# Experts of a mixture in plain fp32 on 32-column tiles of TensorE, 96 places each, in place of split operands on the whole array

## The chip, the cores and the metric

The kernel runs on one core of one Trainium2 chip. The metric is the device time of one execution in microseconds, the median of three. The engines are named as the profile names them: PE is TensorE (PEld its weight loads), DVE VectorE, ACT ScalarE, POOL GpSimd, SP SyncE, which issues the weights' DMAs. All data is float32.

## The reference, cut to what matters

The model has three transformer blocks over 256 tokens of width 1024. The change is in the mixture of experts that ends the second block. Each token takes its two best experts of eight; each expert is a SwiGLU with 3584 hidden units, so `w_in[e]` is 1024 x 7168 (29.4 MB) and `w_out[e]` is 3584 x 1024 (14.7 MB), 352 MB for all eight.

```python
def moe_swiglu(x, w_router, w_in, w_out):
    logits = (xt @ w_router).astype(jnp.float32)
    top_val, top_idx = lax.top_k(logits, TOP_K)
    top_w = jax.nn.softmax(top_val, axis=-1)
    gates = jnp.sum(jax.nn.one_hot(top_idx, N_EXPERTS, dtype=jnp.float32) * top_w[..., None], axis=1)
    y = jnp.zeros_like(xt)
    for e in range(N_EXPERTS):
        y = y + gates[:, e:e + 1] * swiglu(xt, w_in[e], w_out[e])   # (silu(gate) * up) @ w_out
```

With the inputs that are timed the eight experts are chosen by 41, 50, 89, 65, 58, 72, 59 and 78 tokens.

## The kernel before

All large products are made of split operands: a float32 operand x is written as a float32r part h (ACT, L92) and the rest l = x - h (DVE, L93), and x·w becomes h·wh + h·wl + l·wh, three matmuls at TensorE's float32r rate (L161, L162, L164). The weights are split on the core too. `weights` asks for a piece of 1 MB on SP's queue (L108; four buffers `wr` in the pool `raw`), ACT and DVE split it in halves into `wh` and `wl` (four buffers each), and `linear` multiplies. The activations are the stationary operand (128 tokens), the weights are the moving one (512 columns), and the sums stand in the PSUM pool `mm` (three banks). A second PSUM pool, `ps` (five banks), serves everything else.

`moe` first routes: it gives each token a place in its experts' lists, and `pick` makes a 0/1 matrix P of tokens by places. For two experts at a time, `gather` collects the tokens with P as the moving operand (L1028, 2 x 128 places) into `xgh` and `xgl`; `back` transposes P (L1039). Then `expert` runs on 128 places. For each 512 hidden units it makes gate and up, ACT takes silu of the gate (L932), DVE multiplies by up (L934), and TensorE transposes the result (L209, four times 128x128), which is split into `eh` and `el`. The product with `w_out` follows in two halves of 512 columns; each half's result is split into `f`, given back to the tokens by `back`'s transpose (L1077, four matmuls a half) and added to y by DVE (L1078, and L1080 for the statistics after the last expert). The next pair's gather is put into the second expert of a pair, after its second block of hidden units (`midway`). Expert 0's first 512 hidden units are computed over all tokens (`dense`), since they need no list.

A loop at the end (L1102, L1103) repeats the experts for places from 128 on; its count is read from memory, and is 0 for the lists above. The third block begins behind it. The Tile scheduler orders the instructions of each engine; SP's weight loads are in program order.

Of the kernel before, what the change touches and what calls it, by code (L numbers as in the profile page):

```python
# [21 lines left out]
NEG = -1e30  # L22


class K:
    """Shared pools and the operations that several blocks use."""
# [55 lines left out]
    def load(self, dst, src):  # L82
        """A load in the queue of the weights, after those asked for before."""
# [63 lines left out]
            # the short group first, so that the last ones leave the first tile most time ahead of the second  # L147
# [53 lines left out]
    def transpose_split(self, src, t, out, c0, n, pool=None):  # L201
        """Columns 128*c0.. of the token tile src [128, 128 n], into out[c][0|1][:, t]."""
# [11 lines left out]
    def split_tokens(self, x, n=8, pool=None):  # L214
        """x: [128, 2, 128 n] token-major; the split feature-major operand."""
# [11 lines left out]
    def rstd(self, out, var, eps, scale=1.0):  # L227
        """(scale var + eps) ** -0.5 of a few numbers per partition."""
# [26 lines left out]
    def normalize(self, r, stats, eps, gb, out):  # L255
        """out = the normalized rows of r, whose statistics were taken per 512 columns."""
# [11 lines left out]
    def residual_norm(self, x, alpha, eps, gb, out):  # L268
        """Gives evac(t, c0, n, psum) that adds alpha x and after the last columns normalizes."""
# [14 lines left out]
    def ffn(self, xs, w_in, w_out, hidden, make):  # L284
        """(silu(gate) * up) @ w_out, the products handed to what make gives."""
# [27 lines left out]
    def exps(self, sc, rmax, out, ssum):  # L313
        """out = exp(sc - rmax), summed along the row."""
# [22 lines left out]
    def softplus(self, x, shape):  # L337
        """max(x, 0) + log1p(exp(-|x|)), of a few numbers; log1p(e) = log(1 + e) e / ((1 + e) - 1)."""
# [65 lines left out]
def dsa(k, xs, sm, w_in, kv_norm_w, w_uk, w_uv):  # L404
    """The attention over the keys that the index scores choose; its output token-major."""
# [3 lines left out]
    # index keys (on both halves of the partitions) and queries, feature-major  # L409
# [7 lines left out]
    # w_uk with its ranks on the partitions  # L417
# [12 lines left out]
    # normalized latents, feature-major  # L430
# [13 lines left out]
    # keys of the heads, feature-major; values, token-major  # L444
# [23 lines left out]
    # queries, feature-major, scaled  # L468
# [3 lines left out]
    # the keys that each query doesn't attend to: 1  # L472
# [35 lines left out]
    for h8 in range(0, 16, 8):  # L508
        # slope (key - query) [query, head, key - query tile + 128]
# [12 lines left out]
def conv_taps(k, conv_w, conv_b):  # L522
    """Taps and bias with the channels on the partitions."""
# [11 lines left out]
def ssd_conv(k, xs, w_in, cw, xc, half):  # L535
    """silu(causal convolution) of x (half 0), or B and C (half 1), feature-major: eight chunks each."""
# [14 lines left out]
def ssd(k, sm, xc, sz, dt_bias, a_log, d_skip, norm_w):  # L551
    """The scan over two chunks of 128, gated by sz and normalized; token-major."""
# [4 lines left out]
    # dt = softplus(raw + bias) = max(., 0) + log1p(exp(-|.|)), a = -exp(a_log) dt  # L557
# [11 lines left out]
    # running sums within each chunk, and the sum of the first chunk on all partitions  # L569
# [28 lines left out]
    # state after the first chunk, per group [state, 4 heads x 64]  # L598
# [75 lines left out]
def memory_xattn(k, xs, kt, v, w_mq, w_mo, evac, values):  # L674
# [47 lines left out]
    # the four pairs of heads, one stage apart  # L722
# [13 lines left out]
def hybrid_layer(k, x, a):  # L736
    """The first block; x token-major, as its result is."""
# [12 lines left out]
    # dt, c_kv and the weights of the index heads  # L750
# [44 lines left out]
def retention(k, xs, w_in, w_out, evac):  # L795
    """Retention over the whole sequence at once: (q k^T * decay) v per head, normalized and gated."""
# [22 lines left out]
    # decayed scores, keys on the partitions: keys 0..127 x 256 queries, keys 128..255 x 128 queries  # L819
# [37 lines left out]
def stick_breaking(k, xs, w_kv, w_q, w_out, evac):  # L857
    """Stick-breaking attention, keys on the partitions."""
# [34 lines left out]
        # z less the sums of softplus over the keys from each one on  # L893
# [23 lines left out]
def expert(k, xg, w_in, w_out, hidden, evac, first=None, midway=None):  # L917
    """One expert on 128 tokens; evac(c0, n, psum). first, if given, makes the first 512 hidden units;
    midway is called in between."""
    nc = k.nc  # L920
    n = hidden // 128
    hs = []
    for i in range(0, n, 16):
        hs.append(tuple(k.operand(m, 16) for m in ("eh", "el")))
    if first:
        first(hs[0])
    for c0 in range(512 if first else 0, hidden, 512):
        sg = k.w(2, [512], F32, "esg")

        def gate_up(t, c, m, p):  # L930
            if c < hidden:
                nc.scalar.activation(sg, p, AF.Silu)  # L932
            else:
                nc.vector.tensor_tensor(sg, sg, p, op=OP.mult)  # L934
                a = c0 // 128
                k.transpose_split(sg, 0, hs[a // 16], a % 16, 4)

        k.linear(xg, w_in, [[(c0, 512), (hidden + c0, 512)]], gate_up, tiles=1)
        if midway and c0 == 512:
            midway()  # L940
    k.linear([tuple(v[:, :, c % 16] for v in hs[c // 16]) for c in range(n)], w_out, [(0, 512), (512, 512)],
             lambda t, c, m, p: evac(c, m, p), tiles=1)


def moe(k, x, xs, w_router, w_in, w_out, y, before_rest):
    """Adds the gated experts' results to y; each expert works on the tokens sent to it, 128 at a time.
    Gives the statistics of y per 512 columns."""
# [3 lines left out]
    iota = k.load_rows(k.inp["c_iota"], 1, "iota")  # L951
# [4 lines left out]
    # router  # L956
# [19 lines left out]
    # chosen: fewer than two greater logits (of equal ones the first counts as greater)  # L976
# [19 lines left out]
    # place of each token in its experts' lists (far beyond them where it isn't chosen), list lengths  # L996
# [12 lines left out]
    more = small("more", (1,), I32)  # L1009
    nc.vector.tensor_scalar(more, over, 128.5, 8.0, op0=OP.is_gt, op1=OP.mult)  # L1010

    # the tokens in two parts
# [4 lines left out]
    def pick(P, o, col, off):  # L1017
        """P[token, t, o + i] = 1 where the token's place is off + i."""
        for t in range(2):
            nc.vector.tensor_scalar(P[:, t, o:o + 128], iota[:, off:off + 128], col(t), None, op0=OP.is_equal)  # L1020

    def gather(P, n):
        xg = [k.act8(F32R, m) for m in ("xgh", "xgl")]
        for c in range(8):
            p = k.ps.tile([128, 2, 256], F32, name="ps")
            for i in range(2):
                for t in range(2):
                    nc.tensor.matmul(p[:, i, :n], xt[i][:, t, c * 128:c * 128 + 128], P[:, t, :n],  # L1028
                                     start=(i == 0 and t == 0), stop=(t == 1), skip_group_check=True)
            nc.scalar.copy(xg[0][:, c, :n], p[:, 0, :n])  # L1030
            nc.vector.tensor_copy(xg[1][:, c, :n], p[:, 1, :n])
        return xg

    def back(P, o):
        """The transpose of P, [place, token]."""
        pt = k.w(1, [2, 128], F32R, "pback")
        p = k.ps.tile([128, 2, 128], F32, name="ps")
        for t in range(2):
            nc.tensor.transpose(p[:, t], P[:, t, o:o + 128].bitcast(F32), ident)  # L1039
# [473 lines left out]
```

## Time and profile before

| what | value |
|---|---|
| runs | 2670.33, 2671.1 (median), 2671.24 us |
| profiled execution | span 2671.5 us, which is its whole time |
| PE busy, of the span | 98% |
| DVE, ACT busy | 72%, 57% |
| granted TensorE clock, mean of the span | 0.989 |
| HBM read | 623.55 MB |
| first sparse matmul of the experts, last of `w_out` | starts 1420.2 us, 2399.36 us |

The profiled execution stands 0.4 us above the median of the runs. "Busy" counts the time in which at least one instruction of the engine was under way; the matmuls are pipelined, so the time that a stream of them takes is read from the distance of their starts and not from one record's length. A plain float32 matmul is recorded as two records, a float32r one as one.

### The profile page before, as it was taken

The numbers are of one execution on the slowest core, as the hardware profiler recorded it, in microseconds if no ns is written. First come the engines' busy times: TensorE is split into PE (matmuls) and PEld (weight loads), VectorE is DVE, ScalarE is ACT, GpSimd is POOL, SyncE is SP. The second block draws the span as 40 slices with busy tenths as digits, with TensorE's granted clock in tenths as the row PEclk, the third lists the DMA queues.
The fourth block names the chain that finished last, engine by engine and source line by source line (L and its number), as shares of the span: only waits on it lengthen the run. The fifth ranks groups of instructions, "written<-read, shape, count | busy, mean of one in ns | idle before, by whom it ended". The sixth has DMA issues, their size and how long they took to land. (4 is left out here: it accounts for less than half of the span.)

```text
span 2671.5 us, 34975 instructions
## 1 busy us (share of the span) xinstructions
PE 2614.5 (98%) x13305; PEld 2169.4 (81%) x13305; DVE 1933.7 (72%) x2516; ACT 1533.3 (57%) x1987; POOL 60.2 (2%) x82
## 2 busy tenths in 40 slices
PE   8999999999999999999999999999999999998999
PEld 7889888888787987887978888888888888776777
DVE  4555758765555556555478999989999999888665
ACT  4434445444443344443567777777777777765553
POOL 0000000000000000000000000000000000001100
PEclk9999989999999999999999999999999999998999
DMA  7555414453556844655528999999999999987513
GB/s 253 182 168 190 168 49 166 159 188 126 193 180 205 226 158 158 201 181 187 177 95 283 357 340 358 365 356 339 363 360 338 369 359 361 362 309 240 191 64 110
DMA packets 335279, 630.10 MB, mean 236 GB/s; under 512 B 24431, under 2 KB 43136, under 8 KB 334848
## 3 DMA queue, kind: packets, MB, share of 16 engines
q1 hardware_dynamic: 332896, 624.59, 67.3%
q10 hardware_dynamic: 2208, 3.21, 0.9%
q8 instruction: 106, 1.74, 0.3%
q14 instruction: 69, 0.57, 0.1%
HBM read 623.55 MB, written 4.19 MB: 235 GB/s over the span
## 5 line engine op out<-in xcount | busy, mean ns | idle before, releaser
L93 DVE TENSOR_TENSOR wl<-wr,wh 128x1024 fp32r<-128x1024 f32 x1158 | 1374.0, 1218 | 433.2 <-ACT wh L92 404.6
L92 ACT CAST wh<-wr 128x1024 fp32r<-128x1024 f32 x1158 | 1191.2, 1049 | 633.5 <-PE mm L164 454.1
L161 PE MATMUL mm<-wh,xh 128*128 128x512 f32 (+2 forms) x1264 | 492.5, 390 | 7.7 <-ACT xh L92 5.1
L164 PE MATMUL mm<-wh,xl 128*128 128x512 f32 (+2 forms) x1264 | 487.9, 386 | 5.7 <-DVE xl L93 5.7
L162 PE MATMUL mm<-wl,xh 128*128 128x512 f32 (+2 forms) x1264 | 486.8, 386 | 3.8 <-DVE wl L93 3.7
L161 PE MATMUL mm<-wh,xgh 128*128 128x512 f32 x880 | 323.6, 397 | 0.8 <-ACT esg L932 0.5
L162 PE MATMUL mm<-wl,xgh 128*128 128x512 f32 x880 | 322.5, 394 | 0.0
L161 PEld LDWEIGHTS mm<-wh,xh 128*128 128x128 f32 x1264 | 241.0, 191 | 55.5 <-ACT xh L92 8.4
L164 PEld LDWEIGHTS mm<-wh,xl 128*128 128x128 f32 x1264 | 241.0, 191 | 53.6 <-DVE xl L93 8.9
L162 PEld LDWEIGHTS mm<-wl,xh 128*128 128x128 f32 x1264 | 240.8, 191 | 51.7 <-DVE wl L93 8.4
L164 PE MATMUL mm<-wh,xgl 128*128 128x512 f32 x880 | 275.4, 391 | 0.0
L161 PEld LDWEIGHTS mm<-wh,xgh 128*128 128x128 f32 x880 | 165.3, 188 | 50.4 <-ACT esg L932 17.2
L164 PEld LDWEIGHTS mm<-wh,xgl 128*128 128x128 f32 x880 | 165.6, 188 | 34.0
L162 PEld LDWEIGHTS mm<-wl,xgh 128*128 128x128 f32 x880 | 165.5, 188 | 31.9 <-DVE wl L93 0.5
L191 PE MATMUL mm<-xh,wl 128*128 128x256 f32 x648 | 185.7, 287 | 1.4 <-DVE wl L93 1.4
L189 PE MATMUL mm<-xh,wh 128*128 128x256 f32 x648 | 185.9, 287 | 1.2 <-DVE xc L545 0.4
L190 PE MATMUL mm<-xl,wh 128*128 128x256 f32 x648 | 185.5, 286 | 0.4 <-DVE xl L93 0.4
L162 PE MATMUL mm<-wl,eh 128*128 128x512 f32 x448 | 175.0, 391 | 1.1 <-DVE wl L93 1.1
L161 PE MATMUL mm<-wh,eh 128*128 128x512 f32 x448 | 175.6, 392 | 0.0
L164 PE MATMUL mm<-wh,el 128*128 128x512 f32 x448 | 174.7, 390 | 0.0
L189 PEld LDWEIGHTS mm<-xh,wh 128*128 128x128 f32 x648 | 125.6, 194 | 2.2 <-PE ps L209 0.6
L191 PEld LDWEIGHTS mm<-xh,wl 128*128 128x128 f32 x648 | 125.7, 194 | 2.1 <-DVE wl L93 2.0
(450 smaller groups left out, 2922.8 us busy)
## 6 DMA issues: line engine op xcount, KB each, us to landing
wr<-moe_w_in SPq DMA_DIRECT2D x440, 512.0 KB, 6.3
wr<-moe_w_out SPq DMA_DIRECT2D x112, 1024.0 KB, 7.2
wr<-ffn_w_in SPq DMA_DIRECT2D x66, 1024.0 KB, 5.1
wr<-w_in SPq DMA_DIRECT2D x50, 1024.0 KB, 5.1
wr<-ffn_w_out SPq DMA_DIRECT2D x30, 1024.0 KB, 5.1
wr<-ret_w_in SPq DMA_DIRECT2D x24, 1024.0 KB, 5.6
wr<-w_mkv SPq DMA_DIRECT2D x8, 1024.0 KB, 5.0
wr<-w_out SPq DMA_DIRECT2D x8, 1024.0 KB, 5.0
```

Of the source, the lines that this page charges most:

```text
L92: self.nc.scalar.copy(H, src)
L93: self.nc.vector.tensor_tensor(L, src, H, op=OP.subtract)
L161: nc.tensor.matmul(p, h, wh[:, c:c + m], start=first, stop=False)
L162: nc.tensor.matmul(p, h, wl[:, c:c + m], start=False, stop=False)
L164: nc.tensor.matmul(acc[t][i][:rows, :m], l, wh[:, c:c + m], start=False, stop=last)
L189: nc.tensor.matmul(o, wh[:, s], h, start=first, stop=False, skip_group_check=True)
L190: nc.tensor.matmul(o, wh[:, s], l, start=False, stop=False, skip_group_check=True)
L191: nc.tensor.matmul(o, wl[:, s], h, start=False, stop=(k == kn - 1), skip_group_check=True)
```

## The change

Experts have 96 places (`CAP`), in three groups of 32. Inside an expert nothing is split: the gathered tokens `xg`, the hidden units `eh` and the weights are plain float32, and TensorE takes the weights from the DMA's buffer `wr`. A group's 32 places are the stationary operand of a 32-column tile of the array, and the four column tiles at (0, 32j) multiply the same places by four different pieces of the weights: of `w_in` two halves of the gate and two of up, of `w_out` two halves of the columns in each of two row chunks. One matmul into all four tiles is called a set of four below; a piece of 1 MB has three sets, one a group. Sums alternate between three banks of `mm` and three of `ps`; an expert begins with `mm`, has one more accumulator for each 1024 hidden units, and one for `w_out`.

Pieces of `w_in` are 128 rows with 1024 gate and 1024 up columns, in DRAM rows of 4 KB (before: 2 KB); the last half block has 2 KB rows. Pieces of `w_out` are two chunks of 128 rows with all 1024 columns, rows of 4 KB (before 2 KB).

silu and the product now put gate and up, which are on different partitions, together; the transposes are 64 rows by 128 (`turn`, L946), 42 in an expert where there were 28. At an expert's end `evac` adds the two row chunks' sums per group: an ACT copy and two DVE additions of 32x512. Then all 96 places are split (96x1024) and given back with eight matmuls (L1138), as before. Hi and lo products of the gather are summed in PSUM. The loop for longer lists is there twice, for places from 96 and from 192.

```diff
+def expert(k, xg, o, w_in, w_out, hidden, evac, first=None, midway=None):
...
+    def accumulators():
+        banks[0] += 1
+        if banks[0] % 2:
+            return [k.mm.tile([128, 512], F32, name="mm") for _ in range(groups)]
+        return [k.ps.tile([128, 512], F32, name="ps") for _ in range(groups)]
+
+    def turn(g, h, c0, sub):
...
+        for c in range(m):
+            nc.tensor.transpose(p[:, c], h[0:64, c * 128:c * 128 + 128], ident[0:64, 0:64])
+        dst = hidden_units(c0 // 128, 2 * m)[:, :, g * 32:g * 32 + 32].rearrange("p (s c) t -> p c s t", s=2)
+        nc.vector.tensor_copy(dst, p.rearrange("p c (s t) -> p c s t", s=2))
...
+        for c in range(8):
...
+            k.mark = nc.sync.dma_start(raw, src)
+            for g in range(groups):
+                for j in range(4):
+                    nc.tensor.matmul(acc[g][32 * j:32 * j + 32, :sub], xg[:, c, o + 32 * g:o + 32 * g + 32],
+                                     raw[:, j // 2, j % 2 * sub:j % 2 * sub + sub], start=(c == 0), stop=(c == 7),
+                                     tile_position=(0, 32 * j), skip_group_check=True)
+            if c == 3:
+                for f in pend:
+                    f()
+                pend = []
+        for g in range(groups):
+            h = k.wl.tile([128, 1024], F32, name="wl")[:, :512]
+            nc.scalar.activation(h[64:128, :sub], acc[g][0:64, :sub], AF.Silu)
+            nc.vector.tensor_tensor(h[0:64, :sub], h[64:128, :sub], acc[g][64:128, :sub], op=OP.mult)
+            pend.append(partial(turn, g, h, c0, sub))
...
     def run(xg, o, wi, wo, pt, g, last, first=None, midway=None):
...
+            nc.scalar.copy(odd[:64], p[64:128])
+            for c in range(2):
+                nc.vector.tensor_tensor(res[32 * i:32 * i + 32, c], odd[32 * c:32 * c + 32], p[32 * c:32 * c + 32], op=OP.add)
...
+        k.split(f[0][:CAP], f[1][:CAP], made[0][:CAP])
...
+    for r in range(2):
+        k.mark = None
+        n = nc.values_load(more[0:1, r:r + 1], min_val=0, max_val=8)
+        with tc.For_i(0, n, 1) as e:
```

The first place is the end of an expert on PE. Before, in the middle of the product with `w_out`, whose first half of columns is given back between matmuls of the second half:

```order
L161 MATMUL mm<-wh,eh 128x512 [waits Activation_49]
L162 MATMUL mm<-wl,eh 128x512 [waits DVE_49]
L1077 MATMUL ps<-f,pback 128x512 [waits Activation_49]
L1077 MATMUL ps<-f,pback 128x512 [waits PE_49]
L164 MATMUL mm<-wh,el 128x512
L161 MATMUL mm<-wh,eh 128x512
L162 MATMUL mm<-wl,eh 128x512
L164 MATMUL mm<-wh,el 128x512
L161 MATMUL mm<-wh,eh 128x512
L1077 MATMUL ps<-f,pback 128x512 [waits DVE_49]
L1077 MATMUL ps<-f,pback 128x512
```

Now, from the last piece of `w_out` (L983, `mm<-wr,eh`) to the next expert's second piece of `w_in` (L962, `mm<-wr,xg`):

```order
L983 MATMUL mm<-wr,eh 32x512 [waits DMAHW4_49]
L983 MATMUL mm<-wr,eh 32x512 x11
L962 MATMUL mm<-wr,xg 32x512 [waits DMAHW5_49,DVE_49,Activation_49]
L962 MATMUL mm<-wr,xg 32x512 x3
L962 MATMUL mm<-wr,xg 32x512 [waits DVE_49,Activation_49]
L962 MATMUL mm<-wr,xg 32x512 x3
...
L962 MATMUL mm<-wr,xg 32x512 [waits DMAHW6_49]
L1138 MATMUL ps<-wh,pback 128x512 [waits Activation_49]
L1138 MATMUL ps<-wh,pback 128x512 x2
L1138 MATMUL ps<-wl,pback 128x512 [waits DVE_49]
...
L962 MATMUL mm<-wr,xg 32x512 x11
```

Each group's first set of the next expert waits until ACT and DVE have taken the group's old sums out of the same bank; the whole result is given back behind the first matmul, of one tile alone, of the second piece.

The second place is the transposes on PE, between two blocks of hidden units. Before:

```order
L161 MATMUL mm<-wh,xgh 128x512
L162 MATMUL mm<-wl,xgh 128x512 [waits DVE_49]
L161 MATMUL mm<-wh,xgh 128x512
L209 MATMUL ps<-c_ident,esg 128x128 [waits DVE_49]
L209 MATMUL ps<-c_ident,esg 128x128 x3
L162 MATMUL mm<-wl,xgh 128x512
```

Now:

```order
L962 MATMUL ps<-wr,xg 32x512 [waits DMAHW0_49]
L962 MATMUL ps<-wr,xg 32x512 x11
L946 MATMUL ps<-c_ident,wl 128x64 [waits DVE_49]
L962 MATMUL mm<-wr,xg 32x512 [waits DMAHW1_49,Activation_49]
L962 MATMUL mm<-wr,xg 32x512 x3
L962 MATMUL mm<-wr,xg 32x512 [waits Activation_49]
...
L946 MATMUL ps<-c_ident,wl 128x64 x3
L946 MATMUL ps<-c_ident,wl 128x64 [waits DVE_49]
L946 MATMUL ps<-c_ident,wl 128x64 x2
L962 MATMUL mm<-wr,xg 32x512 [waits DMAHW2_49]
```

The four transposes that stood together between matmuls of the same shape stand, in threes and fours or alone, between sets of tiles. Going through an expert in this way, PE leaves the tiles for whole-array or 64-row work 10 times, 14 times where a gather is in it, and twice in an expert that happens behind a single tile's matmul.

## Rows read from the trace of the kernel before

**Rows 1.** The page: span, and busy time of each engine.
```profile
span 2671.5 us, 34975 instructions
PE 2614.5 (98%) x13305; PEld 2169.4 (81%) x13305; DVE 1933.7 (72%) x2516; ACT 1533.3 (57%) x1987; POOL 60.2 (2%) x82
```
**Rows 2.** A window in the experts: PE, PEld, DVE, ACT, POOL; clock, DMA share, GB/s.
```profile
1900.00:2000.00 100.00, 99.95 (x446) 80.43 (x445) 90.93 (x87) 77.05 (x85) 0.00 (x0) 1.00 1.02 362
```
**Rows 3.** Waits from 1600 to 2370 us (6.2 experts): us, times, longest.
```profile
PEld mm L161 <- ACT esg L932: 15.1, 36, 0.9
SPq L108 <- DVE wl L93: 561.4, 263, 5.2
```
**Rows 4.** Line L161 of the experts: ns min/median/max, first and last start.
```profile
L161 PE MATMUL mm<-wh,xgh x880: 386/390/502, 1420.2 to 2357.3; 128*128 128x512 f32 x176
```
**Rows 5.** PE in order of time: two experts' first `w_out` matmul, the last matmuls.
```profile
2236.14 0.39 PE L161 MATMUL mm<-wh,eh 128*128 128x512 f32 x1
...
2358.39 0.39 PE L161 MATMUL mm<-wh,eh 128*128 128x512 f32 x1
...
2395.74 0.39 PE L162 MATMUL mm<-wl,eh 128*128 128x512 f32 x1
...
2399.36 0.39 PE L164 MATMUL mm<-wh,el 128*128 128x512 f32 x1
```
**Rows 6.** Groups of the experts' stretch: busy us, mean ns, idle before.
```profile
L93 DVE TENSOR_TENSOR wl<-wr,wh 128x1024 fp32r<-128x1024 f32 x662 | 776.2, 1221 | 52.3 <-ACT wh L92 42.9
L92 ACT CAST wh<-wr 128x1024 fp32r<-128x1024 f32 x661 | 675.9, 1053 | 127.5 <-PE mm L164 70.7 <-DMA wr<-moe_w_out 31.2 <-DMA wr<-moe_w_in 16.0
```
**Rows 7.** PE in order of time: plain float32, whole array, 512 columns.
```profile
975.41 2.74 PE L840 MATMUL ps<-rv,rst 128*128 128x512 f32 x6
...
978.22 0.39 PE L162 MATMUL mm<-wl,xh 128*128 128x512 f32 x1
```
**Rows 8.** PE: four column tiles (L1354), then 64-row matmuls (L1371).
```profile
2513.84 0.66 PE L1354 MATMUL ps<-cw,ht 128*16 128x64 f32 x32
2514.43 1.07 PE L1371 MATMUL ps<-kct,qkb 64*128 64x16 f32 x16
```
**Rows 9.** PE: whole-array matmuls before and after two column tiles (L909 to L911).
```profile
1357.15 0.39 PE L164 MATMUL mm<-wh,xl 128*128 128x512 f32 x1
1357.47 0.43 PE L909 MATMUL ps<-sbe,sv 128*64 128x128 f32 x2
...
1362.82 0.38 PE L911 MATMUL ps<-sbe,sv 128*64 128x128 f32 x2
1363.13 0.51 PE L161 MATMUL mm<-wh,yh 128*128 128x512 f32 x1
```
**Rows 10.** PE: transposes between the experts' matmuls.
```profile
1671.08 0.60 PE L209 MATMUL ps<-c_ident,esg 128*128 128x128 f32 x4
1671.44 0.48 PE L162 MATMUL mm<-wl,xgh 128*128 128x512 f32 x1
```
**Rows 11.** Windows where most DMA rows are 4 KB, and 8 KB.
```profile
6.00:9.00 3.00, 2.58 (x13) 2.19 (x11) 1.99 (x3) 2.14 (x4) 0.00 (x0) 1.00 1.05 404
275.00:280.00 5.00, 5.00 (x44) 5.00 (x43) 1.96 (x2) 1.99 (x2) 0.00 (x0) 1.00 1.00 416
```
**Rows 12.** All engines in order of time behind the last `w_out` matmul.
```profile
2399.79 0.58 ACT L92 CAST f<-mm 128x512 fp32r<-128x512 f32 x1 [4.18 <-PE mm L164]
2400.41 0.69 DVE L93 TENSOR_TENSOR f<-mm,f 128x512 fp32r<-128x512 f32 x1 [3.35 <-ACT f L92]
...
2401.91 1.41 DVE L1078 SCALAR_TENSOR_TENSOR moe_y<-ps,gate,moe_y 128x512 f32<-128x512 f32 x2
2403.24 1.28 DVE L1080 BATCH_NORM_STATS2 mstats<-moe_y 128x6 f32<-128x512 f32 x2
...
2408.49 0.28 DVE L260 BATCH_NORM_AGGREGATE mv<-mstats 128x2 f32<-128x12 f32 x2 [3.97 <-issue]
...
2413.39 0.90 PE L209 MATMUL ps<-c_ident,h 128*128 128x128 f32 x3 [11.28 <-DVE h L1227]
```

More of the change, by code (lines that the diff above doesn't have):

```diff
@@ L914, in stick_breaking @@
     k.linear(k.pairs(ys, 8), w_out, blocks(0, 1024), evac)
-def expert(k, xg, w_in, w_out, hidden, evac, first=None, midway=None):
+CAP = 96
+def expert(k, xg, o, w_in, w_out, hidden, evac, first=None, midway=None):
     nc = k.nc
+    ident = k.const_in("ident")
+    groups = CAP // 32
     n = hidden // 128
-    hs = []
-    for i in range(0, n, 16):
-        hs.append(tuple(k.operand(m, 16) for m in ("eh", "el")))
+    hs = [k.u8(F32, "eh")[:, :16 * CAP].rearrange("p (c t) -> p c t", c=16) for _ in range(2)]
+    half = 12 if first else 16
+    hidden_units = lambda c, m=1: hs[c >= half][:, c - half * (c >= half):c - half * (c >= half) + m]
@@ L925, in expert @@
     if first:
[L926 to L939, printed above, removed]
-            midway()
@@ L941, in expert @@
-    k.linear([tuple(v[:, :, c % 16] for v in hs[c // 16]) for c in range(n)], w_out, [(0, 512), (512, 512)],
-             lambda t, c, m, p: evac(c, m, p), tiles=1)
+        first(hidden_units(0, 4))
+    banks = [0]
+    def accumulators():
[4 more added lines that the diff above has]
+    def turn(g, h, c0, sub):
+        m = sub // 128
+        p = k.ps.tile([128, m, 64], F32, name="ps")
+        for c in range(m):
+            nc.tensor.transpose(p[:, c], h[0:64, c * 128:c * 128 + 128], ident[0:64, 0:64])
+        dst = hidden_units(c0 // 128, 2 * m)[:, :, g * 32:g * 32 + 32].rearrange("p (s c) t -> p c s t", s=2)
+        nc.vector.tensor_copy(dst, p.rearrange("p c (s t) -> p c s t", s=2))
@@ new lines, in expert @@
+    pend = []
+    starts = list(range(512 if first else 0, hidden, 1024))
+    for c0 in starts:
+        w = min(1024, hidden - c0)
+        sub = w // 2
+        acc = accumulators()
+        for c in range(8):
+            raw = k.raw.tile([128, 2048], F32, name="wr")[:, :2 * w].rearrange("p (g n) -> p g n", g=2)
+            src = w_in[c * 128:c * 128 + 128].rearrange("p (g n) -> p g n", g=2)[:, :, c0:c0 + w]
+            k.mark = nc.sync.dma_start(raw, src)
[7 more added lines that the diff above has]
+                    f()
+                pend = []
+        for g in range(groups):
[3 more added lines that the diff above has]
+            pend.append(partial(turn, g, h, c0, sub))
+        if midway and c0 == starts[1]:
+            midway()
@@ new lines, in expert @@
+    acc = accumulators()
+    for i in range(0, n, 2):
+        raw = k.raw.tile([128, 2048], F32, name="wr").rearrange("p (g n) -> p g n", g=2)
+        k.mark = nc.sync.dma_start(raw, w_out[i * 128:i * 128 + 256].rearrange("(g p) n -> p g n", p=128))
+        for g in range(groups):
+            for j in range(4):
+                c = i + j // 2
+                nc.tensor.matmul(acc[g][32 * j:32 * j + 32], hidden_units(c)[:, 0, 32 * g:32 * g + 32],
+                                 raw[:, j // 2, j % 2 * 512:j % 2 * 512 + 512], start=(i == 0), stop=(i == n - 2),
+                                 tile_position=(0, 32 * j), skip_group_check=True)
+        if i == 6:
+            for f in pend:
+                f()
@@ L945, in moe @@
+    for g in range(groups):
+        evac(g, acc[g])
 def moe(k, x, xs, w_router, w_in, w_out, y, before_rest):
@@ L950, in moe @@
     ident, tri = k.const_in("ident"), k.const_in("tri")
[L951 removed]
+    iota = k.load_rows(k.inp["c_iota"], 2, "iota")
     low = k.load_rows(k.inp["c_low"], 1, "low")
@@ L1058, in first @@
             k.linear(xs, w, [(hidden, 512)], up)
-            for i in range(2):
-                p = k.ps.tile([128, 4, 128], F32, name="ps")
-                for c in range(4):
+            p = k.ps.tile([128, 4, CAP], F32, name="ps")
+            for c in range(4):
+                for i in range(2):
                     for t in range(2):
-                        nc.tensor.matmul(p[:, c], parts[i][:, t, c * 128:c * 128 + 128], P[:, t, 0:128],
-                                         start=(c == 0 and t == 0), stop=(t == 1), skip_group_check=True)
-                (nc.vector.tensor_copy if i else nc.scalar.copy)(h[i][:, 0, 0:4], p)
+                        nc.tensor.matmul(p[:, c], parts[i][:, t, c * 128:c * 128 + 128], P[:, t, 0:CAP],
+                                         start=(c + i + t == 0), stop=(i + t == 2), skip_group_check=True)
+            nc.scalar.copy(h[:, 0:4], p)
         return first
@@ L1070, in run, with evac @@
     def run(xg, o, wi, wo, pt, g, last, first=None, midway=None):
-        def evac(c, m, p):
-            f = k.w(4, [2, 512], F32R, "f")
-            k.split(f[:, 0], f[:, 1], p)
+        made = []
+        def evac(i, p):
+            if not made:
+                made.append(k.w(4, [2, 512], F32, "res"))
+            res = made[0]
+            odd = k.wh.tile([128, 1024], F32, name="wh")[:, :512]
+            nc.scalar.copy(odd[:64], p[64:128])
+            for c in range(2):
+                nc.vector.tensor_tensor(res[32 * i:32 * i + 32, c], odd[32 * c:32 * c + 32], p[32 * c:32 * c + 32], op=OP.add)
+        expert(k, xg, o, wi, wo, hidden, evac, first, midway)
+        f = [v.tile([128, 1024], F32R, name=m).rearrange("p (c n) -> p c n", c=2) for v, m in ((k.wh, "wh"), (k.wl, "wl"))]
+        k.split(f[0][:CAP], f[1][:CAP], made[0][:CAP])
+        for c in range(2):
             for t in range(2):
```

68 lines of the change are left out of this document (33 added, 35 removed).

## The prediction

> **What bounds the kernel now.** I read the page first: PE is busy for 98% of the span, DVE for 72% [rows 1]. That is an average over three blocks, so the window in the experts comes next: PE is never idle at a granted clock of 1.00, DVE stands at 91%, ACT at 77%, and the DMA engines at a share of 1.02 with 362 GB/s [rows 2]. PE and the weights' stream are both at their end here. The waits show which of the two yields: SP's weight loads wait 561 us of 770 for DVE to free a buffer, while PE's own loads wait 15 us in 6.2 experts for the silu [rows 3]. DVE in turn waits for ACT and ACT for PE [rows 6]: the stream is throttled from behind, and its engines show a full share because 2 KB rows are slow in them, not because nothing more could be asked for. The stage runs from 1420.2 us [rows 4] to the last matmul's start at 2399.36 [rows 5], 979.2 us.
>
> One expert takes 122.2 us without a gather (2358.39 - 2236.14). A float32r matmul of 512 columns has a pitch of 3.62 / 16 = 0.226 us [rows 5]. An expert needs (7 blocks x 8 chunks x 2 + 28 chunks x 2) x 3 = 504 of them: 114.0 us. 28 transposes at 0.36 / 4 = 0.09 [rows 10] to 0.108 (0.09 and the 0.08 us by which the next matmul's start is late) are 3.0, eight combining matmuls 1.8. That leaves 3.4 us of waits and late starts, of which the silu wait is 15.1 / 6.2 = 2.4.
>
> **Matmuls of the experts.** Plain float32 goes at half the columns per record and with two records a matmul: from 975.41 to 978.22 lie six records and one float32r matmul, (2.81 - 0.23) / 6 = 0.43 each, so 0.86 us a matmul [rows 7]. Alone that would be 3.8 times the old pitch. Everything hangs on whether four column tiles run together. L1354 is the only place with four: 16 matmuls of 64 columns, 32 records, take 0.66 us [rows 8]. Each tile's four matmuls would take 4 x 0.107 = 0.43 us by the pitch of rows 7; the rest, 0.23, I take for the last record's run-out. One after another they would take 1.7 us. So four run together, at the full pitch of each as far as so short a piece tells. I take 0.86 us for a set of four. An expert has 3 blocks x 8 pieces x 3 groups and 14 x 3 of `w_out`, 114 sets, and 24 sets of half length: 126 x 0.858 = 108.1 us, 5.9 below before. Expert 0 (no half block) gains 5.4. Sum: 7 x 5.9 + 5.4 = **-46.7 us**.
>
> The Trainium skill, "TensorE: Matmul & The Clock Gate", Part 3 on tiles, gives measured speedups that speak against this: 3.07 for four row tiles and 2.38 for three column tiles of 512 columns. A set would then last 4 x 0.858 / 3.07 = 1.12 us, an estimate, and the sum would be 262 us higher. The trace agrees that tiles overlap and cannot exclude the loss, since its only four-tile piece has 64 columns.
>
> **What PE gets in addition.** 42 transposes of 64 rows for 28 of 128. A 64-row matmul of L1371 takes at most 1.07 / 8 = 0.13 us in its row tile [rows 8], the old transposes 0.09 to 0.108. I take 0.111: 4.7 for 3.0 us, **+13.6** for eight experts (with 0.09 to 0.13: +6 to +20).
>
> Changes of tile shape. Going into two column tiles, the first starts 0.32 us behind a matmul whose pitch is 0.23: 0.09 lost. Coming out, 1363.13 stands about 0.20 behind the start of the second of the last two tile records (0.11 us into their row), where a tile's own pitch is 0.05 to 0.11, and the first matmul's record is 0.12 longer than those behind it (0.51 for 0.39) [rows 9]. So a visit elsewhere costs 0.18 to 0.36 us; I take 0.27. With ten visits an expert and four more for each of three gathers that is 92 x 0.27 = **+24.8** (17 to 33).
>
> A tile left alone. Twice in an expert the scheduler puts other work behind the first matmul of a piece, so one tile works 0.86 us while three stand still: 16 x 0.858 = **+13.7**.
>
> The end of an expert. Experts 1 to 7 have five accumulators, so the sum over `w_out` stands in `mm` and the next expert begins in the same three banks. A group's bank is free after an ACT copy (0.58) and two DVE additions, for which the nearest row is 0.69 for 128x512 [rows 12]; with fewer partitions I leave it near that, 0.67. Groups end 0.86 us apart on PE, but DVE needs 1.34 for each: group 0's set waits 1.92 + 0.2 - 2 x 0.86 = 0.4 us, the next two 0.48 more each, 1.4. Six ends (expert 0 ends in `ps`): **+8.6**. If the silu of ACT or the copies of the transposes get between, it can be 3 us each (+18).
>
> **What goes away.** The splits of weights: 776 us of DVE and 676 of ACT [rows 6] leave engines that are not PE's bound; what PE gets back is only its own waits, at most 8 x 3.4 = **-27.2**. I take it all: blocks alternate between two sets of banks, so a block no longer waits for the silu of the one before, and no weight waits for a split. DVE and ACT now have about 25 us of work in 120, which covers the silu, the copies and the giving back, except at an expert's end.
>
> Sum of the stage: -46.7 + 13.6 + 24.8 + 13.7 + 8.6 - 27.2 = **-13.2 us**, 966 us, 120.6 for an expert without a gather.
>
> **The weights' stream.** 42 pieces an expert at 120.6 us leave 2.87 us for each. 4 KB rows ran at 404 GB/s at a share of 1.05, 8 KB rows at 416 [rows 11]; 1.049 MB / 404 = 2.60 us, 109 us an expert, hidden behind PE. At the old 362 GB/s it is 2.90 us, 121.7 an expert. SP now waits for PE alone, whose piece of 2.57 us of work frees a buffer; three others are under way meanwhile, 7.8 us of stream. If PE were faster this cover would be gone at 109 us.
>
> **The end of the stage**, which nothing hides, since the third block's first matmul on PE waits for the normalized tokens [rows 12]. Before, from the last matmul's start to the last statistics: 2404.52 - 2399.36 = 5.2 us, because the first half of the columns was done earlier. After: the additions end about 3.9 us after the last set's start (six of 0.67 on DVE), the cast 96x1024 takes 1.05, the subtraction 1.22 [rows 6], matmuls 0.4, and all eight operations behind them are still to do, 4 x 0.70 + 4 x 0.64 = 5.4 [rows 12]: 12.0 us, **+6.8**. The second loop's count is read like the first's, for which DVE stood 3.97 us [rows 12]: **+4.0** (0 if the two reads overlap, 5 with what surrounds the branch).
>
> Total: -13.2 + 6.8 + 4.0 = -2.4 against the profiled execution's 2671.5, so 2669.1 in its terms; its 0.4 us above the median of the runs is left out of account but for rounding: **2669 us**. Less than 0.2% of the time, 5.3 us, can't be told from no change.
>
> **Rivals.** (A) The sum above, chance 0.70. Its unknown terms (transposes, visits, ends, the waits that may come back with up to 27 us, loop) give it its own range of 2654 to 2690.
>
> (B) The stream bounds: 4 KB rows stay at 362 GB/s beside PE. Then an expert takes 121.7 us at best, and the stalls of PE at its ends aren't made up for, 1 to 3 us each, since only 4 MB are buffered: 8 x 1.1 and 8 x 2, +25 us, 2694. It speaks for it that the share is already 1.02, against it the windows of rows 11, short ones. It decides from 2.87 us a piece. Chance 0.11.
>
> (C) Visits, single tiles and ends cost nothing, because PE's queue lets sets and other work overlap: 47 us less, 2622; the stream at 109 us an expert wouldn't stop it. Against it stand the late starts of rows 9. Chance 0.10.
>
> (D) Four tiles with four different streams of 512 columns are slower than the pitch of one. If the 0.23 us over 0.43 in L1354 were half contention, a set would last 1.27 times as long, 1.09 us: 29 us an expert, +233, 2902. If the array took no more columns in all than the float32r stream, 512 in 0.226 us, two records of four matmuls would need 1.81 us and the kernel 3600. Rows 8 speak against the second (64 columns each 0.014 us, if spread evenly through 0.44). It is the case in which the change is plainly slower; chance 0.09, most of it near 2900. This is where the rule of the skill above would lead.
>
> **Numbers.** Within (A) I give 0.25 to faster by over 5.3 us, 0.27 to within, 0.18 to slower; (B) is slower but for 0.01, (C) faster, (D) slower: faster 0.35, same 0.28, slower 0.37. The range that leaves out (D) and most of (C), and holds (A) and (B): 2635 to 2705.
>
> **What would show it.** In the new profile: the four records of a set start within some 0.05 us of each other and sets follow at 0.86 us; the experts' `w_out` starts are 119 to 123 us apart; DMA at or above 400 GB/s when SP isn't waiting, and SP's waits named PE; PE's idle time at an expert's end 1 to 2 us, behind DVE's additions; two stretches of "issue" before the aggregation of the statistics, and 12 us from the last set to the last statistics. The prediction is wrong if sets follow more slowly, if PE waits for DMA throughout, or if the visits are much cheaper or dearer than 0.27 us.

## The result, and the profile after

The changed kernel takes 2689.5 us (median of seven runs, 2676.4 to 2697.1), the kernel before 2671.1 beside it: 1.0061 times, 95% interval 1.0042 to 1.0081, so about 16 to 18 us slower. The runs of the changed kernel spread over 21 us where those of before spread over 3; the mean granted clock was 0.989 in the fastest of them and 0.984 in the slowest. The profiled execution has a span of 2690.7 us, 19.2 above [rows 1].

The page's head, and the windows of the experts (the first the whole stage, the second that of [rows 2]):

```profile
span 2690.7 us, 42117 instructions
PE 2597.4 (97%) x18071; PEld 1705.7 (63%) x18071; DVE 1201.7 (45%) x1940; ACT 863.3 (32%) x1302; POOL 60.7 (2%) x82
```

```profile
1418.00:2410.00 992.00, 957.90 (x9147) 328.63 (x9149) 152.40 (x273) 78.43 (x140) 0.00 (x0) 0.99 0.94 348
...
1900.00:2000.00 100.00, 94.90 (x917) 33.55 (x910) 19.42 (x33) 9.23 (x16) 0.00 (x0) 0.97 0.94 347
```

DVE and ACT have little to do now, 19 and 9 of 100 us, as the change says. But PE isn't full any more (95 of 100 us), its granted clock is below 1, and the DMA engines move less than before, 348 GB/s at a share of 0.94 for 362 at 1.02 [rows 2]. Neither TensorE nor the stream is at its end over the whole stage: they wait for each other by turns. The stage lasts 992 us from 1418.0 us, 13 more than before, where I had 966; the rest of the 19 us is behind it.

Where PE stops is in the list of waits of PE over the stage, and in its order of time around the start of one `w_out`:

```profile
PE mm L983 <- DMA wr<-moe_w_out: 18.4, 11, 2.9
PE mm L962 <- DVE res L1129: 6.5, 17, 0.4
PE ps L962 <- DMA wr<-moe_w_in: 4.6, 9, 1.0
```

```profile
1603.28 1.50 PE L962 MATMUL ps<-wr,xg 128*32 128x256 f32 x24 [0.18 <-DMA wr<-moe_w_in]
1604.71 0.71 PE L946 MATMUL ps<-c_ident,wl 64*128 64x64 f32 x8
1605.81 0.62 PE L962 MATMUL ps<-wr,xg 128*32 128x256 f32 x2 [0.39 <-DMA wr<-moe_w_in]
1606.36 0.46 PE L946 MATMUL ps<-c_ident,wl 64*128 64x64 f32 x4
1606.75 5.54 PE L962 MATMUL ps<-wr,xg 128*32 128x256 f32 x94
1612.38 0.70 PE L946 MATMUL ps<-c_ident,wl 64*128 64x64 f32 x3
1615.35 4.13 PE L983 MATMUL mm<-wr,eh 128*32 128x512 f32 x24 [2.27 <-DMA wr<-moe_w_out]
```

The rows with 128x256 are the half block at the end of `w_in`, whose pieces are 512 KB. It runs out at 1613, and the first piece of `w_out` isn't there: PE stands still for 2.3 us. Six of the seven experts after the first have such a pause, of 2.2 to 2.9 us. Over the stage the list has 24.6 us of waits of PE for weights: 18.4 and 4.6 above, and two items of 0.8. What the weights and the clock do is seen in windows (columns as in [rows 2]; the first two within the half block, the fourth in the product with `w_out`, the others the four stretches of the stage in which the clock was low):

```profile
1598.00:1608.00 10.00, 9.44 (x146) 5.04 (x142) 3.25 (x6) 1.33 (x3) 0.00 (x0) 1.00 0.85 273
1602.00:1612.00 10.00, 9.44 (x156) 4.96 (x144) 1.28 (x4) 0.45 (x2) 0.00 (x0) 1.00 0.89 304
...
1614.70:1618.10 3.40, 2.75 (x16) 0.91 (x20) 0.00 (x0) 0.00 (x0) 0.00 (x0) 0.50 0.99 394
1618.20:1628.20 10.00, 10.00 (x95) 3.02 (x91) 0.49 (x2) 0.00 (x0) 0.00 (x0) 1.00 0.99 363
1867.30:1874.10 6.80, 5.51 (x26) 1.37 (x27) 0.00 (x0) 0.00 (x0) 0.00 (x0) 0.50 0.99 402
1993.60:2000.40 6.80, 5.88 (x31) 1.61 (x35) 0.19 (x1) 0.00 (x0) 0.00 (x0) 0.50 0.96 390
2372.50:2375.90 3.40, 3.40 (x20) 1.09 (x16) 0.00 (x0) 0.00 (x0) 0.00 (x0) 0.50 1.02 419
```

In the half block the stream falls to 273 and 304 GB/s. Around the end of four of the six pauses PE is granted its lower clock, 1.2 of 2.4 GHz, for 3.4 to 6.8 us: the three sets from 1615.35 take 4.13 us where three and the run-out take 2.7. TensorE worked for 17.5 us at half speed in these stretches, so they cost some 9 us on top of the waits.

The tail, as [rows 12]:

```profile
2404.47 6.19 PE L983 MATMUL mm<-wr,eh 128*32 128x512 f32 x56
...
2409.62 4.14 DVE L1129 TENSOR_TENSOR res<-wh,mm 32x512 f32<-32x512 f32 x6 [32.29 <-ACT wh L1127]
2414.87 1.22 DVE L93 TENSOR_TENSOR wl<-res,wh 96x1024 fp32r<-96x1024 f32 x1 [1.11 <-ACTq L1164]
2416.98 1.41 DVE L1140 SCALAR_TENSOR_TENSOR moe_y<-ps,gate,moe_y 128x512 f32<-128x512 f32 x2 [0.89 <-PE ps L1138]
...
2420.81 1.27 DVE L1142 BATCH_NORM_STATS2 mstats<-moe_y 128x6 f32<-128x512 f32 x2
2426.49 0.28 DVE L260 BATCH_NORM_AGGREGATE mv<-mstats 128x2 f32<-128x12 f32 x2 [4.01 <-issue]
```

From the end of the last `w_out` matmul (2404.47 + 6.19) to the last statistics (2422.08) it is 11.4 us; before it was 4.8 (2399.75 to 2404.52 [rows 5, 12]).

### The profile page after: what moved, and what is told of

The parts are those of the page before. It is cut to its first block, busy times and chain, and to the rows that moved or that the text cites. A ratio compares the mean times of both kernels' runs of the same rounds, so it can differ in the third digit from the quotient of the medians.

```text
span 2690.7 us, 42117 instructions
## 1 busy us (share of the span) xinstructions
PE 2597.4 (97%) x18071; PEld 1705.7 (63%) x18071; DVE 1201.7 (45%) x1940; ACT 863.3 (32%) x1302; POOL 60.7 (2%) x82
## 3 DMA queue, kind: packets, MB, share of 16 engines
q8 instruction: 145, 2.38, 0.3%
HBM read 623.56 MB, written 4.19 MB: 233 GB/s over the span
## 5 line engine op out<-in xcount | busy, mean ns | idle before, releaser
L93 DVE TENSOR_TENSOR wl<-wr,wh 128x1024 fp32r<-128x1024 f32 x494 | 594.9, 1212 | 381.8 <-ACT wh L92 363.0
L92 ACT CAST wh<-wr 128x1024 fp32r<-128x1024 f32 x494 | 512.2, 1044 | 513.1 <-PE mm L164 382.8
L161 PE MATMUL mm<-wh,xh 128*128 128x512 f32 (+2 forms) x1264 | 491.6, 390 | 9.4 <-ACT xh L92 6.8
L962 PE MATMUL mm<-wr,xg 128*32 128x512 f32 x3072 | 346.8, 594 | 7.8 <-DVE res L1129 6.5
L983 PE MATMUL mm<-wr,eh 128*32 128x512 f32 x2352 | 265.0, 608 | 18.5 <-DMA wr<-moe_w_out 18.4
L161 PEld LDWEIGHTS mm<-wh,xh 128*128 128x128 f32 x1264 | 240.3, 190 | 57.7 <-ACT xh L92 10.3
L962 PE MATMUL ps<-wr,xg 128*32 128x512 f32 (+1 forms) x2880 | 261.0, 494 | 4.8 <-DMA wr<-moe_w_in 4.6
L962 PEld LDWEIGHTS mm<-wr,xg 128*32 128x32 f32 x3072 | 98.3, 110 | 232.6 <-issue 211.5
L983 PEld LDWEIGHTS mm<-wr,eh 128*32 128x32 f32 x2352 | 74.8, 112 | 195.7 <-issue 154.3
L962 PEld LDWEIGHTS ps<-wr,xg 128*32 128x32 f32 x2880 | 95.1, 110 | 135.4 <-issue 86.9
L972 DVE TENSOR_TENSOR wl<-wl,mm 64x512 f32<-64x512 f32 x48 | 33.1, 690 | 228.7 <-ACT wl L971 228.7
L1129 DVE TENSOR_TENSOR res<-wh,mm 32x512 f32<-32x512 f32 x42 | 28.5, 679 | 230.3 <-ACT wh L1127 229.6
```

The lines of the kernel that those rows point to most:

```text
L92: self.nc.scalar.copy(H, src)
L93: self.nc.vector.tensor_tensor(L, src, H, op=OP.subtract)
L161: nc.tensor.matmul(p, h, wh[:, c:c + m], start=first, stop=False)
L962: nc.tensor.matmul(acc[g][32 * j:32 * j + 32, :sub], xg[:, c, o + 32 * g:o + 32 * g + 32], raw[:, j // 2, j % 2 * sub:j % 2 * sub + sub], ...
L972: nc.vector.tensor_tensor(h[0:64, :sub], h[64:128, :sub], acc[g][64:128, :sub], op=OP.mult)
L983: nc.tensor.matmul(acc[g][32 * j:32 * j + 32], hidden_units(c)[:, 0, 32 * g:32 * g + 32], raw[:, j // 2, j % 2 * 512:j % 2 * 512 + 512], s ...
```

## The experiments

The question was where the 26 us lie by which the stage exceeds my sum: in TensorE's own work, or in weights that come late. Stage times below run from the first tile matmul to the start of the last record of `w_out`, in each run's profile. The distances of experts are those of the first matmuls of their `w_out`, as in [rows 5].

**TensorE's own pace.** Every second piece of weights is not loaded.

```diff
-            raw = k.raw.tile(...)
...
-            k.mark = nc.sync.dma_start(raw, src)
+            if c % 2 == 0:
+                raw = k.raw.tile(...)
...
+                k.mark = nc.sync.dma_start(raw, src)
...
+        if i % 4 == 0:
             raw = k.raw.tile([128, 2048], F32, name="wr").rearrange("p (g n) -> p g n", g=2)
             k.mark = nc.sync.dma_start(raw, w_out[i * 128:i * 128 + 256].rearrange("(g p) n -> p g n", p=128))
```

> Every second piece of the experts' weights isn't loaded; the piece before it is multiplied again in its place, so half of the experts' products are left out and replaced, and TensorE has the same work with half the stream. Theory S (the stream: TensorE's own sum of about 966 us for the stage holds, and the 26 us above it are waits for weights and the half clock that follows them): the stage from the first tile matmul to the last set of four falls from 992 to 960 to 970 us, no half-clock stretch is left in it, and the whole time is 2655 to 2668. Rival P (TensorE's own work: shape changes, transposes, ends of experts are dearer than summed): the stage stays at 985 to 992 and the time at 2683 to 2692.

2649.9 us (2647.2 to 2653.8), 0.9922 of before (0.9907 to 0.9937). The window over some six experts:

```profile
1600.00:2300.00 700.00, 696.68 (x6798) 241.81 (x6794) 115.48 (x206) 58.01 (x103) 0.00 (x0) 1.00 0.55 186
```

PE is full and at its full clock. The stage takes 949 us, an expert 118.9 without a gather and 122.7 to 123.2 with one. Rival P falls: TensorE's own work isn't dearer than my sum. But not all of the 43 us between 992 and 949 are late weights, because the scheduler ordered TensorE's work differently here: counted from the two traces, PE leaves the tiles for other work 64 times in this stage and 90 times in that of the changed kernel, and at the ends of experts it waits 3.3 us in all, not 6.9. The changed kernel's own 24.6 us of waits for weights and 9 us of half clock make 33 to 34, which leaves at most 959 us for TensorE's own work, 7 less than my 966.

**The stream's own pace.** Only the first group of 32 places is computed.

```diff
-    groups = CAP // 32
+    groups = 1
...
-        k.split(f[0][:CAP], f[1][:CAP], made[0][:CAP])
+        k.split(f[0][:32], f[1][:32], made[0][:32])
...
```

> Only the first 32 places of each list are computed, the other two groups are left out, so TensorE has a third of its work with the whole stream. Theory S: the stream has a pace of its own of 173.5 ns a 4 KB packet and 100.8 a 2 KB one, 2.78 and 3.2 us a MB, 118 us an expert (105 for expert 0): the stage takes 920 to 940 us and the time is 2615 to 2640. Rival (the pace of the windows at the kernel's start, 404 GB/s, 2.60 us a MB): 109 us an expert, stage 850 to 870, time 2545 to 2570.

2586.5 us (2581.9 to 2590.1), 0.9685 of before. An expert takes 113 us (112.4 to 114.5), the stage 888. The window, in which the clock is low because PE waits between pieces:

```profile
1600.00:2200.00 600.00, 400.53 (x2126) 81.19 (x2118) 51.04 (x82) 25.02 (x42) 0.00 (x0) 0.67 1.01 391
```

Neither expectation was met: 391 GB/s lies between 404 (109 us) and the 373 that follow from the packets of the loaded kernel (44 MB in 118 us). The stream with little work on TensorE is faster than TensorE by itself, 113 to 119 us. Over an expert as a whole it could be hidden. In its half blocks it moved only some 300 to 345 GB/s here too, so 113 us isn't the least that it can do.

**Full buffers in the half block.** Two pieces of 512 KB in a buffer of 1 MB.

```diff
-            raw = k.raw.tile([128, 2048], F32, name="wr")[:, :2 * w].rearrange("p (g n) -> p g n", g=2)
+            if w == 1024:
+                raw = k.raw.tile([128, 2048], F32, name="wr").rearrange("p (g n) -> p g n", g=2)
+            elif c % 2 == 0:
+                both = k.raw.tile([128, 2048], F32, name="wr").rearrange("p (c g n) -> p c g n", c=2, g=2)
+                raw = both[:, 0]
+            else:
+                raw = both[:, 1]
```

> In the last half block of an expert two pieces of 512 KB go into one buffer of 1 MB instead of one each, so 4 MB and not 2 are under way there; rows, packets and TensorE's work are the same. Theory S1 (the lead of the stream is lost in the half block because its buffers are half empty): the 2.3 to 2.9 us of waiting before six of seven products with w_out go, with their half-clock stretches, 17 + 7 us: 2663 to 2674. Theory S2 (the stream as a whole is as slow as TensorE, 118 of 121 us, so a lead is never built): the waits move into the product with w_out, and the time stays at 2680 to 2692. Rival P: no change.

2652.6 us (2651.4 to 2659.0), 0.9938 of before (0.9924 to 0.9951): 37 us below the changed kernel, and below the kernel before. The waits on PE and two windows, the second the half block of the same expert as above:

```profile
PE mm L968 <- DVE res L1135: 6.5, 17, 0.4
...
PE mm L989 <- DMA wr<-moe_w_out: 2.9, 6, 1.2
```

```profile
1900.00:2000.00 100.00, 98.92 (x1004) 34.09 (x1000) 13.28 (x27) 6.43 (x12) 0.00 (x0) 1.00 0.98 365
1599.30:1611.20 11.90, 11.90 (x209) 7.07 (x205) 2.60 (x6) 0.98 (x3) 0.00 (x0) 1.00 1.00 362
```

The wait for `w_out` is 2.9 us in the place of 18.4, no half-clock stretch is left in the stage, and the stage takes 957 us. The seven half blocks run at 362 to 392 GB/s, where in the changed kernel they ran at 263 to 306. Rows, packets, bytes and TensorE's work are those of the changed kernel, and so is the order of that work but for a little (87 times away from the tiles for 90). S1 holds; the stage gains 35 us, about what the waits for weights (24.6) and the half clock (9) had cost, above S1's 17 + 7.

**2 KB rows.** The pieces of `w_in` in two DMAs.

```diff
-            k.mark = nc.sync.dma_start(raw, src)
+            for o2 in range(0, w, 512):
+                k.mark = nc.sync.dma_start(raw[:, :, o2:o2 + 512], src[:, :, o2:o2 + 512])
```

> The pieces of w_in are asked for in two DMAs of 512 KB with rows of 2 KB, as before the change, into the same buffers; all else as changed. If the stream is behind the time (S): 24 MB of w_in an expert go from 2.78 to 2.92 us a MB by the packets of before (91.4 ns for 2 KB), 3.4 us an expert, 27 us in all if none of it is hidden: 2700 to 2725. If TensorE's own work sets the time (P): 2685 to 2695, no change.

2702.3 us (2698.4 to 2709.9), 1.0128 of before: 13 us above the changed kernel, at the low end for the stream. But that the stream's rate is behind it isn't shown. PE's listed waits for weights fall from 24.6 to 20.8 us and the half-clock stretches from 20.5 to 13.7, while the stage grows by 6, to 998. The edit halves the rows and also makes two loads of each piece, and a set needs both: tiles 0 and 2 multiply columns of the first load, tiles 1 and 3 of the second. Counted from the starts of the records, one to three of the four tiles stream alone for 56 us of this stage and for 36 of the changed kernel's. The run at the end of this section shows what that looks like.

**The half block first.**

```diff
-    half = 12 if first else 16
+    half = 12
...
-    starts = list(range(512 if first else 0, hidden, 1024))
+    starts = [512 + 1024 * m for m in range(3)] if first else [0, 512, 1536, 2560]
...
-        w = min(1024, hidden - c0)
+        w = 1024 if c0 else 512
```

> As changed, with 512 KB pieces in buffers of their own, but an expert begins with the half block and ends its w_in with a whole one. Theory S1 (what costs is that the half block uses up 4 MB in 10.3 us from half-filled buffers, and that the product with w_out follows it without a pause): the 2.3 to 2.9 us before w_out go, and come back in part behind the half block, where the end of the expert before (1.8 us of waits and 2.5 of giving back) has let the stream run ahead: stage 965 to 980, time 2660 to 2677. Rival (the stream is late for w_out because of w_out's own rows or its place): the waits before w_out stay, 2683 to 2692.

2693.7 us (2689.1 to 2695.2), 1.0082 of before: no gain, and the stage takes 995 us. Neither theory's time was met. PE's waits over the stage:

```profile
PE ps L962 <- DMA wr<-moe_w_in: 17.5, 11, 2.6
PE mm L962 <- DMA wr<-moe_w_in: 10.7, 16, 1.3
```

The waits before `w_out` did go, as S1 said, but came back whole behind the half block, where the second block now begins; the end of the expert before didn't cover them. The wait belongs to the half block wherever it stands, not to `w_out`.

**One loop.** On top of the pairs:

```diff
-    for r in range(2):
+    for r in range(1):
```

> As e3_pairs_of_half_pieces, with the second loop for longer lists left out (places from 192 on aren't computed; no list is that long). By the prediction's term the second loop costs 4.0 us: 2648.5. By the trace after, DVE stands 4.0 us at the loops as it did before with one, and only SP asks for the third block's weights later: 1 to 2 us, 2651.

2650.3 us (2649.3 to 2650.9), 0.9924 of before, 2.2 below e3. DVE stands for 1.82 us ahead of the aggregation, for 4.01 in the changed kernel:

```profile
2385.30 0.28 DVE L260 BATCH_NORM_AGGREGATE mv<-mstats 128x2 f32<-128x12 f32 x2 [1.82 <-issue]
```

The second loop is worth these 2.2 us. Why a single loop costs 1.8 us here and 4.0 in the kernel before stays open.

**Other banks for the next expert.** On top of the pairs:

```diff
+        self.banks = [0]
...
-    banks = [0]
+    banks = k.banks
```

> As e3_pairs_of_half_pieces, with the accumulators alternating on from one expert to the next, so that an expert never begins in the banks that the one before ends in. The three waits of 0.6 us at six ends, 10.6 us, go. Theory E (they are what the end costs): 2642. Rival (the giving back stands behind the first piece and needs the split result, 5.3 us after the last set; what isn't waited for in front of the first piece is waited for there): 2650 to 2655, no change beside e3.

2667.7 us (2659.0 to 2673.1), 0.9983 of before: 15 us above e3, worse than either theory. The list of waits and one end in PE's order of time:

```profile
PE ps L1145 <- ACT wh L93: 15.3, 6, 4.2
```

```profile
1653.58 1.22 PE L1145 MATMUL ps<-wh,pback 96*128 96x512 f32 x2 [4.24 <-ACT wh L93]
1654.84 1.22 PE L1145 MATMUL ps<-wl,pback 96*128 96x512 f32 x2
...
1657.69 4.87 PE L969 MATMUL ps<-wr,xg 128*32 128x512 f32 x40
```

The waits in front of the next expert's sets are gone, but the edit also moved other work. At three of the seven ends between experts the scheduler put the giving back (L1145) directly behind the last set of `w_out`, as here, where the next expert's first set stands behind it at 1657.69; in e3 the first piece stood in between. So PE waits the whole 4.24 us for ACT, three times. At the other four ends the first piece is still in front, and the wait is 0.86 us or less, where the three short waits of an end had cost 1.7: there the rival is half right. The long pauses bring the lower clock too: two matmuls of 512 columns take 1.22 us there for some 0.6, and TensorE works 19 us of the stage at half speed, a loss of nearly 10. These two things make e7 slower than e3, not the other banks.

**And the giving back later.** On top of e7, the split and the eight matmuls are put behind the next expert's fourth piece. e8 has one loop, e9 both.

```diff
             if c == 3:
-                for f in pend:
+                for f in pend + k.late:
                     f()
...
+        def finish():
+            f = [v.tile([128, 1024], F32R, name=m)...]
...
+        if last:
+            finish()
+        else:
+            k.late.append(finish)
```

> As e7_pairs_other_banks, with one loop and with the giving back put behind the fourth piece of the next expert in the program. If the ends' waits are only that, nothing is left to wait for at an end: 10.6 us for the ends and 1 to 2 for the loop below e3: 2638 to 2643. If the stream (113 us an expert by itself) is what stands behind them, PE waits for weights instead: 2647 to 2652.

> As e8 with the two loops of the changed kernel, and each expert's result is weighted with its own gates also where it is given back late (in e8 the late ones were weighted with the next expert's gates). Nothing is left out. The time is that of e8 and the second loop, 2643 + 2 to 4: 2645 to 2647; against the kernel before 0.989 to 0.992. If the late giving back had only seemed free in e8, 2650 or more.

e8: 2643.0 us (2638.6 to 2644.5), 0.9898 of before. e9: 2645.7 us (2638.7 to 2648.2), 0.9900 (0.9886 to 0.9915). This is the fastest complete version. Its window:

```profile
1600.00:2300.00 700.00, 696.44 (x6868) 238.85 (x6862) 120.07 (x211) 59.84 (x106) 0.00 (x0) 1.00 0.99 371
```

PE and the stream are both at their end; the stage takes 944 us. Nothing is waited for at an expert's end any more. Part of the gain is again the order: a tile is left alone 6 times in the stage, 16 times in e3.

**2 KB rows with full buffers.** e3 with the loads of e4.

> As e3_pairs_of_half_pieces, with the pieces of w_in asked for in rows of 2 KB (two DMAs a piece). It tells what the 4 KB rows are worth once the buffers are full. If the stream is hidden now (PE 119 us an expert): 2652 to 2657, no change beside e3. If it is close to the bound, 122 us an expert by 91.4 ns a packet: some 13 to 25 us above e3, 2666 to 2678.

2669.3 us (2662.8 to 2673.1), 0.9991 of before, 17 above e3. The window:

```profile
1600.00:2300.00 700.00, 691.27 (x6648) 248.22 (x6644) 114.32 (x203) 56.35 (x103) 0.00 (x0) 1.00 0.97 358
```

At a share of 0.97 as in e3 these rows bring 358 GB/s for e3's 364. PE's listed waits for weights are 2.9 us, less than e3's 4.0, so the 17 us aren't there. They are where a set stands with some of its tiles only, as here, in expert 0:

```profile
1443.55 0.59 PE L969 MATMUL ps<-wr,xg 128*32 128x512 f32 x1
1443.82 0.61 PE L969 MATMUL mm<-wr,xg 128*32 128x512 f32 x3
1443.98 0.59 PE L969 MATMUL ps<-wr,xg 128*32 128x512 f32 x1
1444.81 1.50 PE L969 MATMUL ps<-wr,xg 128*32 128x512 f32 x12 [0.24 <-DMA wr<-moe_w_in]
```

One tile begins a piece of the next block at 1443.55, the other three at 1444.81, when the second load is there; only 0.24 us of this count as waiting. One to three tiles stream alone for 52 us of this stage and 34 of e3's; in whole sets that is a loss of 27 and 16 us, so 11 of the 12 us by which the profiled stages differ (970 and 957). Asking for the pieces in two loads with 2 KB rows costs 13 to 17 us in e4 and here; whether by the rows or by the second load isn't shown, since no run changed one alone.

## Why the prediction was wrong

The forecast was 2669 us, no change; the time is 2689.5, within the range but 18 us slower, on the other side of the kernel before. That it also lies within (A)'s own 2654 to 2690 is luck: TensorE's own work came out below the sum, and what lies above it are late weights, which (A) put at nothing.

**The step that failed** is the weights' stream, "2.60 us, 109 us an expert, hidden behind PE". Two things were wrong in it. Its size: with little work on TensorE the stream takes 113 us an expert (e2), and beside full TensorE work it moves 364 to 371 GB/s at shares of 0.97 to 0.99 (e3, e9), not 404. And its form, which mattered more: I compared means over an expert and counted "three others under way, 7.8 us of stream" as cover everywhere. In the half block a buffer holds 0.5 MB. There the sets take 8 x 1.29 = 10.3 us for 4 MB, and the four buffers hold 2 MB, so the stream falls to about 290 GB/s and needs 14 us (4.19 MB / 0.29). What is lost there PE waits for at the next full-speed stretch, and the lower clock adds to it. e3 changes the buffers alone and gives back 37 us; e5 shows that it isn't `w_out`. Rival (B) gave about the right time, 2694, by luck too, for a stream at 362 GB/s that bounds on the average; e1 and e2 show that on the average TensorE's 119 us are the longer ones, e3 that even 364 GB/s is nearly enough when the buffers are full.

**The sets of four** were right. 56 records in 6.19 us are seven sets, 0.86 each with 0.16 of run-out taken off. Rival (D) is out. The Trainium skill, "TensorE: Matmul & The Clock Gate", Part 3 on tiles, has a measured speedup of 2.38 for three column tiles of 512 columns. For a stream of sets this trace doesn't agree: four different streams take 0.86 us where one takes 0.858 [rows 7], about 4.0 for four.

**Transposes** were too dear, and **visits** were right. In the order of time above four transposes and the way back take 0.39 us from their start to the next tiles (1606.36 to 1606.75), and they start 0.55 us behind the start of a matmul of 256 columns, which takes 0.43 (1605.81 to 1606.36): 0.12 are lost on the way in. In the same place of e3:

```profile
1604.61 0.70 PE L946 MATMUL ps<-c_ident,wl 64*128 64x64 f32 x8
1605.24 0.62 PE L968 MATMUL ps<-wr,xg 128*32 128x256 f32 x2
1605.79 0.46 PE L946 MATMUL ps<-c_ident,wl 64*128 64x64 f32 x4
1606.18 5.16 PE L968 MATMUL ps<-wr,xg 128*32 128x256 f32 x91
```

Four take 0.39 and eight 0.63: 0.06 each and 0.15 for the way back, with the 0.12 for the way in 0.27 a visit, as I had it; a transpose has half of my 0.111. 330 transposes take 20 us where I had 37, the 90 visits of the trace some 24 where I had 25. So rival (C), by which visits cost nothing, falls.

**The end of an expert** was right in its mechanism: sets start at 1655.37, 1656.82 and 1658.22 for 0.86 us each, behind DVE's additions,

```profile
1655.37 1.06 PE L962 MATMUL mm<-wr,xg 128*32 128x512 f32 x8 [0.43 <-DVE res L1129]
1656.82 1.06 PE L962 MATMUL mm<-wr,xg 128*32 128x512 f32 x8 [0.38 <-DVE res L1129]
1658.22 1.88 PE L962 MATMUL mm<-wr,xg 128*32 128x512 f32 x10 [0.34 <-DVE res L1129]
```

1.45 - 0.86 = 0.59 and 1.40 - 0.86 = 0.54 us are lost between them, and 0.43 and the run-out of 0.16 ahead of the first: 1.7 us an end, for 1.4 (six times 1.4 is 8.4, not 8.6). It isn't a cost that the other banks alone take off (e7); with the giving back put off as well it goes (e9).

**The rest of the sum.** A tile is left alone 16 times, as I had it, but seven of the pieces have 256 columns: 9 x 0.86 + 7 x 0.43 = 10.7 us for 13.7. TensorE's own work takes at most 959 us (the changed kernel without waits for weights and half clock), and 953 by e3 without its 4 us of waits: 7 to 13 below 966, where transposes, visits, tiles left alone and ends together are some 19 below my prices. So the other terms gave some 6 to 12 us less than I took. The waits that go, -27.2, were taken whole; which of them came back wasn't measured apart.

**The tail**: 11.4 for 4.8 us, +6.6 where I had +6.8. **The second loop**: 2.2 us (e6) for 4.0; from the last statistics to the aggregation it is 4.4 us with two loops (2422.08 to 2426.49) and 4.0 before with one.

Put together for the profiled execution: the stage +13 (for -13), its start 2 us earlier, the tail and the loop +8.5 (for +10.8), 19 us in all.

## What to carry to other kernels

Whether a stream is hidden is read for each stretch with its own demand and its own bytes under way, not for the mean of a stage: count MB in the buffers, not buffers. TensorE needed no more per MB in the half block than elsewhere (1.29 us for 0.5 MB, 2.57 for 1 MB); it broke there because the pieces filled half of their buffers, and PE waited at the next stretch. A wait taken out of one place is only gained if the work behind it has cover elsewhere: e7 took 10 us of waits away and was 15 slower, since the giving back came to stand where nothing covered it, and e9 gained when it was put off. And an edit can change the scheduler's order of all the rest: compare the orders of two traces before their difference is put down to the edit (e1, e4, e7, e10).

## What the hardware showed that I had not expected

Four 32-column tiles with four different streams of plain fp32 run at the full pace of each (0.86 us a set). A 64-row transpose between them costs 0.06 us, and the way there and back 0.27. Four of the six pauses of TensorE ahead of `w_out` (2.3, 2.8, 2.7 and 2.8 us) came with a granted clock of 0.50 for 3.4 to 6.8 us, so that a short wait for data is paid again; the other two (2.2 and 2.9 us) didn't, nor did the many waits of 0.4 us in e3. And four buffers with 0.5 MB in each let the stream fall to 263 to 306 GB/s, where the same rows in full buffers ran at 362 to 392.
